# Conformer convolution on one core: six channel tiles convolved by TensorE from shifted copies, and w_mod tiles shared out anew

## The chip, the cores and the metric

The kernel runs on 1 core of one Trainium2 chip. The metric is the device time of that core for one execution, in microseconds (us).

## What is computed

A trunk of two layers over 256 positions and 2048 channels, all in float32. The change lies in layer 0, whose mixer is the conformer module:

```python
def conformer_conv(u, w_pw1, b_pw1, w_dw, b_dw, ln_g, ln_b, w_pw2, b_pw2):
    v = u @ w_pw1 + b_pw1                      # 2048 -> 4096
    a, gt = jnp.split(v, 2, axis=-1)
    v = a * jax.nn.sigmoid(gt)
    v = causal_dwconv(v, w_dw, b_dw)           # 31 taps, each channel by itself
    v = jax.nn.silu(layernorm(v, ln_g, ln_b))  # over the 2048 channels
    return v @ w_pw2 + b_pw2

sc = jax.nn.silu(c)
for i in range(2):
    mod = (sc @ w_mod[i] + b_mod[i])[:, None, :]          # w_mod[i]: 2048 x 12288
    sh1, sc1, g1, sh2, sc2, g2 = jnp.split(mod, 6, axis=-1)
    u = rmsnorm(h, norm_mix_g[i]) * (1 + sc1) + sh1
    h = h + g1 * mix(u)                                   # conformer, then Mamba-2
    u = rmsnorm(h, norm_mlp_g[i]) * (1 + sc2) + sh2
    h = h + g2 * sq_relu_mlp(u, mlp_w1[i], mlp_w2[i])
return rmsnorm(h, final_norm_g)
```

## The kernel before

Activations lie transposed: 128 channels on the partitions, the 256 positions along the row. The 2048 channels are 16 **tiles** of 128, in four groups of four.

**First pointwise product** (`native`, L635). Its 4096 output columns are eight blocks; block b holds the halves a and gate of tiles 2b and 2b + 1. Blocks 0 to 2 run together, blocks 3 to 7 one by one, each in four quarters with a weight of 1 MB (16 products at L649; a float32 product stands as two records in the profile). When a block ends, `glu` (L563) writes its two gated tiles into a ring of 12 padded tiles, `vpad`, in the spare half of the buffers `u`.

**Convolution** (`conv`, L572). The first tile's begins at block 3; from block 4 on, three tiles go into each block. A tile's 31 taps are shared: ScalarE multiplies 24 (L580), four at a time into one wide buffer; VectorE adds the wide buffers (five adds of 128 x 1024, L596), adds seven taps by itself (L599) and folds the four lanes into one (L603, L605). For tiles 14 and 15 TensorE does 13 taps with diagonal weights (L592), ScalarE 12 and VectorE 6. `close` (L608) subtracts the channel mean of tile 0 (made at L614 between the second and the third quarter of block 3; L617), so that later sums stay small, and squares the result.

**Normalisation.** `moments` (L624, L631) sums tiles and squares of a group over the channels, with products of 32 output columns, four of them beside each other; groups 0 to 2 go this way. L730 adds the three groups' rows, L737 the four tiles of the last group; VectorE reads the mean off the bank (L740), and `normed` turns group after group into what the second product reads.

**Second pointwise product** (`outer` and `block`, products at L355). Its weights are split into a high part (ScalarE, L340) and a low part (VectorE, L342).

**w_mod.** The gate and shift vectors are needed step by step, so their matrix (96 MB a layer) is streamed all along in 1 MB **w_mod tiles** of 128 columns, `gemv`. On VectorE a tile is one multiply and sum (L271); on TensorE it is four products of 32 output columns with the conditioning vector as weight (L262), and after four tiles a row copy by ScalarE (L268) and a **turn** of the row into columns (four transposes, L283). `PE_GROUPS` names the groups of tiles that TensorE does, `EARLY` sets the order of the tiles, and `pump(n)` starts n of them: 16 in the 20 quarters of blocks 3 to 7 (`RATE_PW1`), 8 between the products (`BETWEEN`), 16 in the second product (`RATE_PW2`), 8 in the opening of the MLP (`RATE_OPEN`). G1 is the gate behind the conformer, SC2 and SH2 scale and shift ahead of the MLP; each has four groups of four tiles.

**Order of the work.** SyncE (SP) issues all weight loads from one queue in program order (`stream`, L324), each when its buffer is free: `w32` has 3 buffers, `wm` 2, `hid` 4, `acc` 5. On the other engines a scheduler orders by program order and priority: `high_priority(n)` moves an instruction ahead, `issue_after(x)` puts it behind x. PSUM has six banks `mm` and two `ms`.

Of the kernel before, what the change touches and what calls it, by code (L numbers as in the profile page):

```python
# [29 lines left out]
def spread(n, slots):  # L30
# [17 lines left out]
BETWEEN = 8  # L48
# [47 lines left out]
def layout(inp):  # L96
# [5 lines left out]
    head[:HEADS, 1] = a["mb_a_log"].reshape(-1)  # L102
    par = np.concatenate([
# [3 lines left out]
        _cols(a["cf_b_dw"]), _cols(a["cf_ln_g"]), _cols(a["cf_ln_b"]), _cols(a["cf_b_pw2"]),  # L107
# [22 lines left out]
    return {  # L130
        "diag": diag,
# [5 lines left out]
        "pw1": _tiles(pw1), "pw2": _tiles(a["cf_w_pw2"][0]),  # L137
# [23 lines left out]
class Trunk:  # L161
# [368 lines left out]
    def conformer(self):  # L530
# [32 lines left out]
        def glu(ct, bank):  # L563

            with self.tc.high_priority(AHEAD_GLU):
# [3 lines left out]
                nc.vector.scalar_tensor_tensor(out=vpad[ct % 12][:, TAPS - 1:], in0=bank[:, :T],  # L569
                                               scalar=self.col("b_pw1", ct), in1=sg, op0=ALU.add, op1=ALU.mult)  # L570

        def conv(ct):  # L572
# [4 lines left out]

# [9 lines left out]
            if few:  # L587
                i = ct - (NT - DIAG)
                part = (self.bank(self.mm, "mm") if i else self.bank(self.ms, "ms"))[:, :T]
                with self.tc.issue_after(self.pe):  # L590
                    for k in range(PE_TAPS):
                        nc.tensor.matmul(part, lhsT=diag[i][:, k, :], rhs=vp[:, k:k + T], start=k == 0,  # L592
                                         stop=k == PE_TAPS - 1)
# [12 lines left out]
            return y  # L606

        def close(ct, y):  # L608
# [26 lines left out]
        def native(blocks, done, pump=None, hook=None):  # L635
# [67 lines left out]
        native([FIRST], glu, pump=pump, hook=lambda: close(0, y))  # L703
        ct = 1
        for b in range(FIRST + 1, 8):
            for _ in range(3):
                close(ct, conv(ct))
                ct += 1
            if b >= 6:
                moments(b - 6)  # L710
            if b == 7:
                self.rings = ("wm", "hid")
                diag = []
                for i in range(DIAG):
                    diag.append(self.b("hid", [P, PE_TAPS, P]))
                    self.stream(diag[i], a["diag"][i])
# [582 lines left out]
```

## Time and profile before

| | |
|---|---|
| median of 3 runs | 2610.97 us (2608.09 to 2614.57) |
| profiled execution, time | 2609.13 us |
| its span | 2607.2 us, mean granted clock 0.988 |
| TensorE busy (PE) | 2541.3 us, 97% |
| weight loads (PEld) | 2180.5 us, 84% |
| VectorE busy (DVE) | 1945.7 us, 75% |
| ScalarE busy (ACT) | 1363.9 us, 52% |
| moved by DMA | 659.10 MB, mean 253 GB/s |

The profiled execution lies 1.8 us under the median. Times in the rows below are microseconds from the start of the span. PEclk is the share of full speed that TensorE's clock was granted, where 1.00 is 2.4 GHz. SPq is SyncE issuing a DMA. `mm` and `ms` are PSUM banks, `wm` and `hid` buffers of w_mod tiles, `w` a weight, `acc` and `sq` a closed tile and its square. A busy share near 1 of TensorE in a stretch says that it sets the pace there; a bracket at a row's end gives the idle time ahead of it and what ended it.

### The profile page before, as it was taken

What the parts mean: (1) busy time and instruction counts of PE and PEld (TensorE: products, weight loads), DVE (VectorE), ACT (ScalarE), POOL (GpSimd) and SP (SyncE); (2) the same over time, 40 slices, a digit from 0 to 9 for tenths busy, and PEclk for the clock granted to TensorE, in tenths of its full rate; (3) what the DMA queues carried; (4) which work ended last, traced back from release to release, by engine and by line L of the source; (5) the groups of instructions that cost most, each with busy time, mean ns of one, the idle gap of its engine ahead of it and who ended that gap; (6) DMA issues with size and microseconds to landing.
All of it is one profiled execution on the core that took longest, in us unless ns stands there. A gap on an engine that the chain in (4) does not pass through costs nothing.

```text
span 2607.2 us, 36320 instructions
## 1 busy us (share of the span) xinstructions
PE 2541.3 (97%) x14291; PEld 2180.5 (84%) x14291; DVE 1945.7 (75%) x2558; ACT 1363.9 (52%) x2145; POOL 132.5 (5%) x170
## 2 busy tenths in 40 slices
PE   6999999999999999999999999999999999999998
PEld 4877798888888888888888888888998888888886
DVE  6689977677888878887877777888885565565565
ACT  2099754444434434447777666744454344443443
POOL 0000000000000000000000000000000101101000
PEclk8999999999999999999999999999999999999999
DMA  9876797588888888866555455688775555555553
GB/s 406 345 278 252 279 376 285 218 337 320 314 323 328 314 307 334 312 225 220 182 188 184 166 182 182 234 305 317 285 263 189 192 193 190 185 191 194 187 186 144
DMA packets 92878, 659.10 MB, mean 253 GB/s; under 512 B 10497, under 2 KB 10497, under 8 KB 14753
## 3 DMA queue, kind: packets, MB, share of 16 engines
q1 hardware_dynamic: 89138, 644.53, 65.6%
q0 software_dynamic: 3136, 10.59, 1.4%
q8 instruction: 112, 1.84, 0.3%
q10 hardware_dynamic: 432, 1.66, 0.2%
q14 instruction: 60, 0.49, 0.1%
HBM read 654.53 MB, written 2.20 MB: 252 GB/s over the span
## 4 chain that ended last, share of the span: by engine, by line
PE 87%; DVE 6%; DMA 3%; ACT 2%; issue 1%; POOL 0%; ACTq 0%; DVEq 0%; SPq 0%; POOLq 0%
PE mm L355 57%; PE mm L409 8%; PE mm L411 8%; PE mm L410 8%; PE mm L649 3%; ACT taps L580 2%; DMA hid<-wmT 1%; DVE taps L596 1%; DVE wl L342 1%; DVE taps L599 1%; DMA wm<-wmT 1%; DVE hid L271 1%; DVE wm L271 1%; PE ms L262 1%; DMA t<-eac_d 0%
## 5 line engine op out<-in xcount | busy, mean ns | idle before, releaser
L355 PE MATMUL mm<-u,wh 128*128 128x512 f32 (+1 forms) x4544 | 1376.1, 365 | 6.9 <-ACT u L467 3.4
L342 DVE TENSOR_TENSOR wl<-w,wh 128x1024 fp32r<-128x1024 f32 x768 | 940.7, 1228 | 513.5 <-ACT wh L340 510.3
L340 ACT CAST wh<-w 128x1024 fp32r<-128x1024 f32 x768 | 806.8, 1051 | 980.6 <-PE mm L355 602.5
L355 PE MATMUL mm<-u,wl 128*128 128x256 f32 x3840 | 1078.9, 282 | 0.1
L355 PEld LDWEIGHTS mm<-u,wh 128*128 128x128 f32 x4544 | 812.8, 190 | 160.2 <-issue 12.8
L355 PEld LDWEIGHTS mm<-u,wl 128*128 128x128 f32 x3840 | 729.8, 190 | 6.6 <-issue 2.5
L409 PE MATMUL mm<-wh,hid 128*128 128x512 f32 x896 | 350.7, 391 | 0.0
L411 PE MATMUL mm<-wh,hid 128*128 128x512 f32 x896 | 348.8, 389 | 0.0
L410 PE MATMUL mm<-wl,hid 128*128 128x512 f32 x896 | 348.7, 389 | 0.0
L271 DVE SCALAR_TENSOR_TENSOR wm<-wm,scb 128x2048 f32<-128x2048 f32 x128 | 292.3, 2283 | 8.2 <-DMA wm<-wmT 8.2
L649 PE MATMUL mm<-u,w 128*128 128x256 f32 x1024 | 232.3, 388 | 26.7 <-ACT u L560 25.1
L649 PEld LDWEIGHTS mm<-u,w 128*128 128x128 f32 x1024 | 197.6, 195 | 64.9 <-ACT u L560 26.6
L409 PEld LDWEIGHTS mm<-wh,hid 128*128 128x128 f32 x896 | 168.2, 188 | 35.7 <-issue 1.0
L410 PEld LDWEIGHTS mm<-wl,hid 128*128 128x128 f32 x896 | 168.2, 188 | 35.4 <-issue 0.7
L411 PEld LDWEIGHTS mm<-wh,hid 128*128 128x128 f32 x896 | 168.2, 188 | 35.2
L355 PE MATMUL mm<-hid,wh 128*128 128x512 f32 (+1 forms) x576 | 182.5, 373 | 2.4 <-DVE acc L837 2.4
L580 ACT ACTIVATE taps<-u,par 128x256 f32<-128x256 f32 x360 | 148.2, 500 | 3.6 <-DVE taps L596 2.2
L355 PE MATMUL mm<-hid,wl 128*128 128x256 f32 x512 | 143.8, 281 | 0.0
L355 PEld LDWEIGHTS mm<-hid,wh 128*128 128x128 f32 x576 | 104.1, 188 | 23.1 <-DVE acc L837 2.7
L299 POOL TENSOR_TENSOR mod<-mod,par 128x4 f32<-128x4 f32 x46 | 39.8, 864 | 1319.3 <-DVE wm L271 885.1
L355 PEld LDWEIGHTS mm<-hid,wl 128*128 128x128 f32 x512 | 96.9, 189 | 0.4 <-issue 0.2
L596 DVE TENSOR_TENSOR taps<-taps,taps 128x1024 f32<-128x1024 f32 x74 | 90.1, 1218 | 8.7 <-ACT taps L580 7.8
(241 smaller groups left out, 1562.9 us busy)
## 6 DMA issues: line engine op xcount, KB each, us to landing
w<-w SPq DMA_DIRECT2D x256, 1024.0 KB, 4.9
wm<-wmT SPq DMA_DIRECT2D x140, 1024.0 KB, 7.0
w<-win SPq DMA_DIRECT2D x80, 1024.0 KB, 4.9
hid<-wmT SPq DMA_DIRECT2D x52, 1024.0 KB, 10.6
w<-pw SPq DMA_DIRECT2D x48, 1024.0 KB, 5.3
w<-wout SPq DMA_DIRECT2D x32, 1024.0 KB, 6.9
acc<-ac_d POOLq DMA_DIRECT2D x16, 512.0 KB, 7.7
h<-xT SPq DMA_DIRECT2D x4, 512.0 KB, 6.2
```

The costliest lines, as they stand in the source:

```text
L262: self.pe = nc.tensor.matmul(self.row_sums[32 * t:32 * t + 32, :], lhsT=self.scol[:, kt:kt + 1].broadcast_to([P, 32]), rhs=w[:, t * 512:(t ...
L271: self.sum = nc.vector.scalar_tensor_tensor(out=w, in0=w, scalar=1.0, in1=self.scb, op0=ALU.mult, op1=ALU.mult, accum_out=m[:, i:i + 1]).ins
L299: nc.gpsimd.tensor_tensor(out=m, in0=m, in1=b, op=ALU.add)
L340: nc.scalar.copy(out=wh, in_=w[:, s, :])
L342: nc.vector.tensor_tensor(out=wl, in0=w[:, s, :], in1=wh.bitcast(F32), op=ALU.subtract)
L355: self.pe = self.nc.tensor.matmul(out, lhsT=lhsT, rhs=rhs, skip_group_check=True, **kw).ins
L409: mm(banks[q], lhsT=hi, rhs=wh[:, k, :], start=g == 0 and t == 0, stop=False)
L410: mm(banks[q], lhsT=hi, rhs=wl[:, k, :], start=False, stop=False)
L411: mm(banks[q], lhsT=lo, rhs=wh[:, k, :], start=False, stop=g == 3 and t == 3)
L580: st["tap"] = nc.scalar.activation(out=p4[:, q, :], in_=vp[:, k + q:k + q + T], func=AF.Identity, scale=self.col("w_dw", ct * TAPS + k + q ...
L596: nc.vector.tensor_add(wide, wide, products(four("wl"), k))
L649: self.pe = nc.tensor.matmul(o, lhsT=w[:, t, j * P:(j + 1) * P], rhs=u[g][:, t, :], start=g == 0 and t == 0 and j < 2, stop=g == 3 and t == 3,
```

## The change

1. **Six tiles are convolved by TensorE, all 31 taps** (`TE_ROWS`: tiles 3, 4, 5, 13, 14, 15; a *convolved tile*). `shift` copies the padded tile four times by DMA, each 8 positions on: 128 rows of 263 values become 32 partitions with four channels each (*copies*: 512 pieces of 1,052 bytes a tile). `weigh` loads the tile's weights (0.5 MB). `convolve` makes 32 products: a product takes 32 channels, a quarter of the output partitions, and four taps, which are 8 apart. The last tap, the 32nd, is zero, so padded tiles are one column longer. `close` takes the result from PSUM and adds the bias in the same instruction. The channels of these six tiles come out permuted; the parameters and the rows of pw2 are permuted to match.
2. **Weights and copies have one buffer each** (`quad` on `acc`, `copies` on `xpad`) for tiles 3, 4, 5, 13 and 14; tile 15 has its own. They are asked for at quarter 2 of blocks 3, 4 and 5 and quarter 3 of block 7; the convolution stands in quarter 3, ahead of its products. Half of the copies of tiles 14 and 15 is issued from ScalarE's queue.
3. **The other ten tiles** have 28 taps on ScalarE (six adds) and three on VectorE.
4. **The end of the conformer is written out:** FILL (three w_mod tiles), convolution 14, moments of group 2, sums of tiles 12 and 13, convolution 15, the row of sums, sums of 14 and 15, mean.
5. **w_mod:** only SH2's tiles are TensorE's now, G1's are VectorE's; `EARLY` brings SH2's first eight tiles forward, and three tiles are started in FILL, five in BETWEEN.

```diff
-BETWEEN = 8
+FILL, BETWEEN = 3, 5
-ACT_TAPS = 24
-DIAG, PE_TAPS, FEW_TAPS = 2, 13, 12
-EARLY = [(0, s, g) for s, g in ((G1, 0), (G1, 1), (G1, 2), (SC2, 0), (G1, 3), (SH2, 0), (SC2, 1), (SH2, 1), (SC2, 2),
-                               (SH2, 2), (SC2, 3), (SH2, 3))]
-PE_GROUPS = {(0, G1, g) for g in range(4)} | {(0, SH2, g) for g in range(4)}
+ACT_TAPS = 28
+TE_ROWS = (3, 4, 5, 13, 14, 15)
+LONG = T + 7
+EARLY = [(0, s, g) for s, g in ((G1, 0), (G1, 1), (G1, 2), (SC2, 0), (SH2, 0), (SH2, 1), (G1, 3), (SC2, 1), (SH2, 2),
+                               (SC2, 2), (SH2, 3), (SC2, 3))]
+PE_GROUPS = {(0, SH2, g) for g in range(4)}
...
+    taps = np.zeros((32, D), f)
+    taps[:TAPS] = a["cf_w_dw"][0].reshape(TAPS, D)
+    quad = np.zeros((len(TE_ROWS), 4, 32, 8, 4, 32), f)
+    for i, ct in enumerate(TE_ROWS):
+        w = taps[:, ct * P:(ct + 1) * P].reshape(4, 8, 32, 4)
+        for p in range(32):
+            quad[i, :, p, :, :, p] = w[:, :, p, :]
...
-        W = T + TAPS - 1
+        W = T + TAPS
...
+            nc.gpsimd.memset(v[:, W - 1:], 0.0)
...
+        quad = self.b("acc", [P, 8, P], bufs=5)
+        copies = self.xpad[:, :4 * LONG].rearrange("p (c t) -> p c t", c=4)
...
+        def weigh(ct, w):
+            self.stream(w, a["quad"][TE_ROWS.index(ct)])
+        def shift(ct, r):
+            for i in range(4):
+                dst, src = r[32 * i:32 * i + 32], vpad[ct % 12][:, 8 * i:8 * i + LONG]
+                if ct >= NT - 2 and i % 2:
+                    with self.tc.high_priority(AHEAD_CHAIN):
+                        nc.scalar.dma_start(out=dst, in_=src)
+                else:
+                    self.stream(dst, src)
+        def convolve(ct, w, r):
+            o = parts[ct] = self.bank(self.mm, "mm")[:, :T]
+            with self.tc.issue_after(self.pe):
+                for k in range(8):
+                    for c in range(4):
+                        self.pe = nc.tensor.matmul(o[32 * c:32 * c + 32, :], lhsT=w[:, k, 32 * c:32 * c + 32],
+                                                   rhs=r[:, c, k:k + T], start=k == 0, stop=k == 7,
+                                                   skip_group_check=True).ins
...
+            if ct in parts:
+                self.sub = nc.vector.scalar_tensor_tensor(out=d, in0=parts[ct], scalar=self.col("b_dw", ct),
+                                                          in1=st["m0"], op0=ALU.add, op1=ALU.subtract).ins
...
+                    if row and g == (3 if row == 13 else 2):
+                        weigh(row, quad)
+                        shift(row, copies)
                     load(0, g)
                     self.pump(pump(g))
+                    if row and g == 3:
+                        convolve(row, quad, copies)
+                        if row == 13:
+                            weigh(14, quad)
                     products(0, g, 0, 4)
...
+        native([FIRST], glu, pump=pump, hook=lambda: close(0, y), row=3)
+        for b, rows in ((4, (1, 2, 3)), (5, (4, 6, 7)), (6, (5, 8, 9)), (7, (10, 11, 12))):
+            for ct in rows:
+                close(ct, None if ct in parts else conv(ct))
             if b >= 6:
                 moments(b - 6)
...
+            native([b], glu, pump=pump, row={4: 4, 5: 5, 7: 13}.get(b))
+        there = [self.load_w(a["pw2"][0, 0])]
+        self.side = self.ms, "ms"
+        with self.tc.issue_after(self.pe):
+            self.pump(FILL)
...
+        shift(14, copies)
+        quad15 = self.wp.tile([P, 8, P], F32, tag="wh", name=self.nm("taps"), bufs=3)
+        weigh(15, quad15)
+        copies15 = self.b("hid", [P, 4, LONG])
+        shift(15, copies15)
+        there.append(self.load_w(a["pw2"][1, 0]))
+        close(13, None)
+        convolve(14, quad, copies)
         moments(2)
...
+        with self.tc.issue_after(self.pe):
+            direct(12, first=True)
+            direct(13)
+        convolve(15, quad15, copies15)
+        close(14, None)
+        close(15, None)
...
+            direct(14)
+            direct(15)
```

How instructions stand on three engines shows what the text of the diff does not. On VectorE at the start of the convolution, where tile 0 is summed (`taps_595` and `taps_609` are tile 0's wide buffer, `taps_746` and `taps_790` tile 1's), the order was:

```order
L596 TENSOR_TENSOR taps_595<-taps_595,taps_618 128x1024
L596 TENSOR_TENSOR taps_595<-taps_595,taps_624 128x1024
L599 SCALAR_TENSOR_TENSOR taps_595<-u_161,par,taps_595 128x256 x7
L596 TENSOR_TENSOR taps_746<-taps_746,taps_751 128x1024
L603 TENSOR_TENSOR taps_595<-taps_595 128x512
L596 TENSOR_TENSOR taps_746<-taps_746,taps_757 128x1024
L605 TENSOR_TENSOR taps_595<-taps_595 128x256
L596 TENSOR_TENSOR taps_746<-taps_746,taps_763 128x1024
L596 TENSOR_TENSOR taps_746<-taps_746,taps_769 128x1024
L617 TENSOR_TENSOR acc_177<-taps_595,ssum_687 128x256
```

There, seven taps follow the last add of tile 0. The same place on VectorE is now, with `wm_677` a w_mod tile:

```order
L604 TENSOR_TENSOR taps_609<-taps_609,taps_632 128x1024
L282 SCALAR_TENSOR_TENSOR wm_677,mod_679<-wm_677,scb 128x2048
L604 TENSOR_TENSOR taps_609<-taps_609,taps_638 128x1024
L604 TENSOR_TENSOR taps_609<-taps_609,taps_644 128x1024
L607 SCALAR_TENSOR_TENSOR taps_609<-u_162,par,taps_609 128x256 x3
L604 TENSOR_TENSOR taps_790<-taps_790,taps_795 128x1024
L609 TENSOR_TENSOR taps_609<-taps_609 128x512
L604 TENSOR_TENSOR taps_790<-taps_790,taps_801 128x1024
L611 TENSOR_TENSOR taps_609<-taps_609 128x256
L604 TENSOR_TENSOR taps_790<-taps_790,taps_807 128x1024
L651 TENSOR_TENSOR acc_190<-taps_609,ssum_699 128x256
```

The seven single taps of tile 0 have become three, the adds one more, and a w_mod tile of 128 x 2048 stands between them, ahead of the two folds (L609, L611) that end tile 0's sum.

On TensorE in the tail, the rows from the last moments' tiles to the second product were (`hid_1643` and `hid_1645` are diagonal weights, `t_268` the row of sums):

```order
L631 MATMUL ms_1379<-sq_1539,ones 32x256
L631 MATMUL ms_1379<-sq_1586,ones 32x256
L592 MATMUL ms_1806<-u_161,hid_1643 128x256 x13
L592 MATMUL mm_1851<-u_162,hid_1645 128x256 x13
L730 MATMUL mm_1894<-t_268_1849,bT_116 128x512
L737 MATMUL mm_1894<-acc_180,ones 128x256
L737 MATMUL mm_1894<-lo_1633,ones 128x256
L737 MATMUL mm_1894<-acc_180,ones 128x256
L737 MATMUL mm_1894<-nrm_1804,ones 128x256
L737 MATMUL mm_1894<-acc_180,ones 128x256
L737 MATMUL mm_1894<-lo_1847,ones 128x256
```

Both convolutions stood together there, ahead of all sums. TensorE's rows are now, from the last quarter of block 7 on (`acc_194` is `quad`, `xpad` its copies; the first L634 is tile 13, then 14, then 15):

```order
L634 MATMUL mm_1684<-xpad,acc_194 32x256 x32
L683 MATMUL mm_1605<-u_165,w_239_1676 128x256 x8
L683 MATMUL mm_1606<-u_165,w_239_1676 128x256 x8
L273 MATMUL ms_1745<-hid_1742,scol 32x512 x4
L273 MATMUL ms_1745<-hid_1750,scol 32x512 x4
L273 MATMUL ms_1745<-wm_1756,scol 32x512 x4
L634 MATMUL mm_1780<-xpad,acc_194 32x256 x32
L665 MATMUL ms_1351<-acc_192,ones 32x256 x4
```

Three w_mod tiles (L273) stand ahead of convolution 14 where the moments stood. Behind four more rows of moments TensorE goes on with the first sums of the last group:

```order
L773 MATMUL mm_1823<-acc_193,ones 128x256
L773 MATMUL mm_1823<-lo_1595,ones 128x256
L773 MATMUL mm_1823<-acc_193,ones 128x256
L773 MATMUL mm_1823<-nrm_1778,ones 128x256
L634 MATMUL mm_1828<-hid_1770,taps_1768 32x256 x32
L784 MATMUL mm_1823<-t_255_1821,bT_117 128x512
L773 MATMUL mm_1823<-acc_193,ones 128x256
L773 MATMUL mm_1823<-lo_1862,ones 128x256
```

The sums of tiles 12 and 13 now stand ahead of convolution 15, the row of sums and those of tiles 14 and 15 behind it.

On SyncE's queue, from the last quarter of block 7 on, the loads were:

```order
L326 DMA w_251_1719<-pw 128x2048
L326 DMA wm_1721<-wmT 128x2048
L326 DMA w_275_1896<-pw 128x2048
L326 DMA w_276_1898<-pw 128x2048
L326 DMA w_277_1900<-pw 128x2048
L326 DMA hid_1941<-wmT 128x2048
L326 DMA wm_1949<-wmT 128x2048
```

They are weights and w_mod tiles alone. SyncE's loads are now:

```order
L337 DMA acc_194<-quad 128x1024
L337 DMA xpad<-u_162 32x4x263 x4
L337 DMA w_239_1676<-pw 128x2048
L337 DMA wm_1678<-wmT 128x2048
L337 DMA acc_194<-quad 128x1024
L337 DMA w_244_1740<-pw 128x2048
L337 DMA hid_1742<-wmT 128x2048
L337 DMA hid_1750<-wmT 128x2048
L337 DMA wm_1756<-wmT 128x2048
L337 DMA xpad<-u_162 32x4x263 x2
L337 DMA taps_1768<-quad 128x1024
L337 DMA hid_1770<-u_163 32x4x263 x2
L337 DMA w_252_1775<-pw 128x2048
```

Where three pw2 weights and the w_mod tiles stood, the weights of tile 14 (the second `acc_194`) stand ahead of a pw2 weight, three w_mod tiles and half of tile 14's copies (the second `xpad`).

## Rows read from the trace of the kernel before

**Rows 1.** Busy time by stretch: us, busy of each engine, PEclk, DMA share, GB/s.
```profile
131.00:293.00 162.00, 160.34 (x814) 127.74 (x812) 153.40 (x234) 154.84 (x385) 8.03 (x9) 1.00 0.67 257
293.00:320.00 27.00, 22.25 (x128) 14.66 (x120) 23.34 (x41) 17.89 (x40) 0.00 (x0) 1.00 0.80 316
320.00:425.00 105.00, 104.99 (x858) 95.28 (x858) 75.35 (x97) 52.62 (x80) 7.83 (x10) 1.00 0.91 360
```

**Rows 2.** Timeline of TensorE, the tail: start, us, line, [idle before <-releaser].
```profile
292.23 0.64 PE L631 MATMUL ms<-acc,ones 128*32 128x256 f32 x8
292.69 0.61 PE L631 MATMUL ms<-sq,ones 128*32 128x256 f32 x8
293.23 5.88 PE L592 MATMUL ms<-u,hid 128*128 128x256 f32 x26
...
310.02 0.70 PE L737 MATMUL mm<-acc,ones 128*128 128x256 f32 x2 [1.84 <-DVE acc L617]
...
317.89 1.06 PE L262 MATMUL ms<-wm,scol 128*32 128x512 f32 x8 [2.30 <-DMA wm<-wmT]
...
320.01 0.39 PE L355 MATMUL mm<-u,wh 128*128 128x256 f32 x1 [0.62 <-DVE u L465]
```

**Rows 3.** Timeline of VectorE, the tail.
```profile
309.54 0.42 DVE L617 TENSOR_TENSOR acc<-taps,ssum 128x256 f32<-128x256 f32 x1
...
311.20 0.42 DVE L740 TENSOR_SCALAR a<-mm 128x256 f32<-128x256 f32 x1
```

**Rows 4.** Timeline of TensorE, blocks 3 to 7.
```profile
135.90 7.14 PE L649 MATMUL mm<-u,w 128*128 128x256 f32 x32 [1.66 <-DMA w<-pw]
142.97 1.06 PE L262 MATMUL mm<-wm,scol 128*32 128x512 f32 x8
143.97 7.17 PE L649 MATMUL mm<-u,w 128*128 128x256 f32 x32
...
191.81 0.66 PE L283 MATMUL mm<-ident,t 128*128 128x128 f32 x4
```

**Rows 5.** Groups by line, 318 to 425 us: weight loads of w_mod (busy, mean ns).
```profile
L262 PEld LDWEIGHTS ms<-hid,scol 128*32 128x32 f32 x48 | 0.9, 106 | 0.8
```

**Rows 6.** Timeline of VectorE, tile 0.
```profile
141.56 1.23 DVE L596 TENSOR_TENSOR taps<-taps,taps 128x1024 f32<-128x1024 f32 x1 [0.37 <-ACT taps L580]
...
144.42 2.86 DVE L599 SCALAR_TENSOR_TENSOR taps<-u,par,taps 128x256 f32<-128x256 f32 x7
...
150.07 0.42 DVE L605 TENSOR_TENSOR taps<-taps 128x256 f32<-128x256 f32 x1
```

**Rows 7.** Groups by line of VectorE, 131 to 320 us.
```profile
L596 DVE TENSOR_TENSOR taps<-taps,taps 128x1024 f32<-128x1024 f32 x74 | 90.1, 1218 | 8.7 <-ACT taps L580 7.8
L599 DVE SCALAR_TENSOR_TENSOR taps<-u,par,taps 128x256 f32<-128x256 f32 x110 | 45.1, 477 | 0.4
...
L271 DVE SCALAR_TENSOR_TENSOR hid<-hid,scb 128x2048 f32<-128x2048 f32 x2 | 4.6, 2281 | 0.0
```

**Rows 8.** Groups by line of ScalarE, 131 to 320 us.
```profile
L580 ACT ACTIVATE taps<-u,par 128x256 f32<-128x256 f32 x360 | 148.2, 500 | 3.6 <-DVE taps L596 2.2 <-DVE u L569 1.5
```

**Rows 9.** The page's DMA queues, and one issue in SyncE's timeline.
```profile
q1 hardware_dynamic: 89138, 644.53, 65.6%
q0 software_dynamic: 3136, 10.59, 1.4%
...
313.08 0.33 SPq L326 DMA_DIRECT2D wm<-wmT  x1
```

**Rows 10.** TensorE by slices; six slices from 430 to 436, first and last.
```profile
316.00:318.00 2.00, 0.11 (x4) 1.00 1.00 406
...
430.00:431.00 1.00, 0.39 (x2) 0.50 0.44 90
...
435.00:436.00 1.00, 1.00 (x7) 0.50 0.99 418
```

**Rows 11.** w_mod's products alone (L262) in the second product.
```profile
320.00:425.00 105.00, 10.64 (x80) 1.56 (x80) 1.00 0.91 360
```

More of the change, by code (lines that the diff above doesn't have):

```diff
@@ L102, in layout @@
     head[:HEADS, 1] = a["mb_a_log"].reshape(-1)
+    order = np.arange(D).reshape(NT, P)
+    for ct in TE_ROWS:
+        order[ct] = order[ct].reshape(32, 4).T.reshape(-1)
+    order = order.reshape(-1)
     par = np.concatenate([
@@ L106, in layout @@
         a["cf_w_dw"][0].reshape(TAPS, NT, P).transpose(2, 1, 0).reshape(P, -1),
-        _cols(a["cf_b_dw"]), _cols(a["cf_ln_g"]), _cols(a["cf_ln_b"]), _cols(a["cf_b_pw2"]),
+        *(_cols(np.asarray(a[n]).reshape(-1)[order]) for n in ("cf_b_dw", "cf_ln_g", "cf_ln_b")), _cols(a["cf_b_pw2"]),
         a["mb_conv_w"][0].reshape(4, 48, P).transpose(2, 1, 0).reshape(P, -1),
@@ L136, in layout @@
         "wmT": wmt,
-        "pw1": _tiles(pw1), "pw2": _tiles(a["cf_w_pw2"][0]),
+        "pw1": _tiles(pw1), "pw2": _tiles(a["cf_w_pw2"][0][order]),
         "wdt": np.ascontiguousarray(wdt.reshape(NT, P, P).transpose(1, 0, 2)),
@@ L586, in conv @@
             four = lambda tag: self.wp.tile([P, 4, T], F32, tag=tag, name=self.nm("taps"), bufs=3)
[L587 to L593, printed above, removed]
             wide = products(four("wh"), k0)
@@ L633, in moments, with native @@
                                          skip_group_check=True)
-        def native(blocks, done, pump=None, hook=None):
+        def native(blocks, done, pump=None, hook=None, row=None):
             banks = [[self.bank(self.mm, "mm") for _ in range(2)] for _ in blocks]
@@ L710, in conformer @@
                 moments(b - 6)
[L711 to L716, printed above, removed]
-            native([b], glu, pump=pump)
+            native([b], glu, pump=pump, row={4: 4, 5: 5, 7: 13}.get(b))
[3 more added lines that the diff above has]
+            self.pump(FILL)
@@ L718, in conformer @@
         with self.tc.issue_after(st["gate"]):
             nc.scalar.activation(out=self.t("rcol", [P, 2])[:, :1], in_=self.eps, func=AF.Sqrt)
-        moments(2)
-        while ct < NT:
-            close(ct, conv(ct))
-            ct += 1
-            if ct == NT - 1:
-                rows = self.t("t2", [P, 2 * T], bufs=3)
-                nc.scalar.copy(out=rows, in_=st["sums"])
+        shift(14, copies)
+        quad15 = self.wp.tile([P, 8, P], F32, tag="wh", name=self.nm("taps"), bufs=3)
@@ new lines, in conformer, with direct @@
+        weigh(15, quad15)
[4 more added lines that the diff above has]
+        convolve(14, quad, copies)
+        moments(2)
+        rows = self.t("t2", [P, 2 * T], bufs=3)
+        nc.scalar.copy(out=rows, in_=st["sums"])
+        ps = self.bank(self.mm, "mm")
+        def direct(i, first=False):
+            for e in range(2):
+                self.pe = nc.tensor.matmul(ps[:, e * T:(e + 1) * T], lhsT=self.ones, rhs=st["sq"][i][e],
+                                           start=first and e == 0, stop=i == NT - 1, skip_group_check=True).ins
@@ L727, in conformer @@
+        with self.tc.issue_after(self.pe):
[4 more added lines that the diff above has]
+        close(15, None)
         tap, d15 = st["tap"], self.sub
-        ps = self.bank(self.mm, "mm")
         with self.tc.issue_after(self.pe):
-            nc.tensor.matmul(ps, lhsT=self.sel, rhs=rows, start=True, stop=False, skip_group_check=True)
-        there = [self.load_w(a["pw2"][b, 0]) for b in range(3)]
+            nc.tensor.matmul(ps, lhsT=self.sel, rhs=rows, start=False, stop=False, skip_group_check=True)
@@ L734, in conformer @@
         with self.tc.high_priority(AHEAD_CHAIN):
-            for i in range(12, NT):
-                for e in range(2):
-                    self.pe = nc.tensor.matmul(ps[:, e * T:(e + 1) * T], lhsT=self.ones, rhs=st["sq"][i][e], start=False,
-                                               stop=i == NT - 1, skip_group_check=True).ins
+            direct(14)
+            direct(15)
             mean, var, msq = (self.t("a", [P, T], bufs=3) for _ in range(3))
@@ L773, in conformer @@
             half = self.split_half(there[0], 0, tap, d15)
-        self.side = self.ms, "ms"
         with self.tc.issue_after(self.pe):
             self.pump(BETWEEN)
+        there.append(self.load_w(a["pw2"][2, 0]))
         self.rings = ("wm", "hid", "hid")
@@ L987, in mamba @@
         self.time_steps(u)
-        self.xpad = [self.one.tile([P, 3 + T], F32, tag=f"xpad{i}", name=f"xpad{i}") for i in range(5)]
+        self.xpad = [self.xpad[:, i * (3 + T):(i + 1) * (3 + T)] for i in range(5)]
         for v in self.xpad:
```

26 lines of the change are left out of this document (8 added, 18 removed).

## The prediction

> **What bounds the kernel now.** I read the busy time by stretch first: it says which engine sets the pace in each stage. From 131 to 293 us, the first pointwise product with its gate and the convolution, TensorE is busy 160 of 162 us while VectorE and ScalarE are busy 153 and 155 [rows 1]: three engines run level. From 320 to 425 us, the second pointwise product, TensorE alone is full and VectorE has 30 us to spare [rows 1]. Between them lies the **tail**, which this change is about, so I read TensorE's timeline there: its last block of products ends at 292.23, then it convolves 13 taps of tiles 14 and 15 (from 293.23), waits 1.84 us for VectorE's last tile, starts the last sums at 310.02, and goes over to the second product at 320.01 [rows 2]. VectorE's timeline shows why: it closes tile 15 at 309.54 and takes the mean at 311.20 [rows 3]. So ahead of the tail the price of an edit is its time on TensorE; in the tail it is what the last two tiles wait for; after 320 it is TensorE again.
>
> My zero, Z, is the end of block 7 on TensorE, 292.23 before. The mean was taken at Z + 19.0, the second product ran at Z + 27.8.
>
> **Blocks 3 to 7 (136 to 292 us).** TensorE loses the twelve w_mod tiles of G1's groups 0 to 2, 1.00 us each from the start of one to the products behind it [rows 4], 12.0 us; and three turns of a row into columns, 0.5 each (the one at 191.81 and its like) [rows 4], 1.5 us. It gains four convolved tiles (3, 4, 5, 13). No row has this convolution, but the moments have its shape: products of 32 output columns over 256 positions, four side by side. Their first eight records start at 292.23, the next eight at 292.69 [rows 2]: 0.46 us for four products. A tile has 32 products, eight such rounds, 3.7 us; four tiles 14.8. Upper bound, if the four did not run side by side: 64 records at 0.22 (32 records in 7.1 us) [rows 4], 14 us a tile. I take 3.7, the nearest row; w_mod tiles, with four different weights, run side by side too. Net **+1.3 us**.
>
> A rule speaks against it. In the moments' rows sixteen records with sixteen weight loads of about 0.11 us [rows 5] pass in 0.92 us, so the loads hide. The Trainium skill ("TensorE: Matmul & The Clock Gate", Part 3 on packing small matmuls) says that a weight load overlaps running products only when its row group differs, and products placed side by side by output columns share theirs. By it the loads would add up, as in the third rival below; no run here has these very weights.
>
> A new wait comes with it. TensorE makes the mean of tile 0 after the second quarter of block 3, and all its work queues behind. Before, tile 0 was summed at 150.5 [rows 6], and TensorE, held 1.00 by a w_mod tile, asked at 151. Now it asks at 135.90 + 2 x 7.04 = 150.0 [rows 4]. VectorE has six adds and three taps now instead of five and seven, but a w_mod tile stands between adds 4 and 5 (order of VectorE). Add 4 ends at 142.8 [rows 6]; w_mod tile 2.3 [rows 7] to 145.1; two adds to 147.4; three taps at 0.41 [rows 7] to 148.6; and the four instructions that then end the sum took 147.2 to 150.5 before [rows 6], so 151.9 now. ScalarE's four extra taps, 0.41 each [rows 8], are done by then. TensorE stands **+2.0 us**; bounds 0, if the w_mod data let the adds go first on time, and 3.
>
> VectorE and ScalarE are relieved: ten tiles instead of fourteen and two part ones. Adds and taps of VectorE: 10 x (6 x 1.22 + 3 x 0.41) = 85 us against 135 [rows 7], plus twelve w_mod tiles, 27. ScalarE: 280 taps, 115 us against 148 [rows 8]. None of it shortens the path: TensorE's 156 us cover both, and VectorE's added w_mod tiles with them. Copies and weights of tiles 3, 4, 5 and 13, 1 MB a tile, are asked for a quarter block or more ahead with the DMA engines at 0.67 [rows 1]: nothing. So Z moves by +3.3.
>
> **The tail.** SP's queue sets it. The weights of tile 14 reuse tile 13's buffer, so SP waits for convolution 13, which ends one quarter block, 7.0 us, before Z. Behind it stand a pw2 tile, three w_mod tiles (FILL) and half of tile 14's copies. One megabyte alone, issued at 313.08, was of use to TensorE at 317.89, 4.8 us [rows 2, 9]; each further one adds 2.5 us at 418 GB/s [rows 10]. With 4.7 MB the third w_mod tile is there at Z - 6.7 + 2.3 + 11.3 = Z + 6.9. Meanwhile ScalarE's queue sends its half of the copies through the same engines. A copied tile is 512 pieces of 1,052 bytes. Lower bound by bytes: q1's mean packet is 7,231 bytes and 307 ns (65.6% of 16 engines' span, by its 89,138 packets), so 45 ns. Upper bound: q0's mean packet, 3,377 bytes, 186 ns [rows 9]. The line through the two gives 113 ns, which I take: 512 x 113 / 16 engines = 3.6 us a tile, 1.8 a queue. ScalarE's halves put the third w_mod tile off to some Z + 9, and tile 14's last copies follow 1.8 later: Z + 10.8. TensorE's order is FILL, convolution 14, moments, sums of 12 and 13, convolution 15, the rest: until Z + 10.8 it has only FILL's 3 us to do.
>
> From there: convolution 14 3.7, moments 0.9, sums of 12 and 13 1.8 (eight records at 0.22), to Z + 17.2; tile 15's weights and copies, 4 us behind tile 14's, are there; convolution 15 3.7; the row of sums and the sums of 14 and 15, 2.6, with closing and squaring 15 alongside. Mean at **Z + 23.4 against Z + 19.0: +4.4**. With pieces at 45 ns it is +2.3, at 186 ns +9.5; if TensorE never waited, its own work is 15.7 and the term -3.3. From the mean to the second product 8.8 us stay.
>
> **The second product.** Ten w_mod tiles stood in TensorE's way there, 80 records [rows 11]; the new order leaves five (one of BETWEEN, four of SH2's third group): **-5.0**. Three turns before, three now. VectorE gets four more tiles, 9 us, where it has 30 free [rows 1]; the last stands just ahead of the last evacuation and could cost up to 1 us. In the MLP's opening the same eight tiles change places: 0, bounds -0.5 and 2. Zeroing one more column per padded tile fills idle GpSimd time: 0.
>
> **Sum:** 1.3 + 2.0 + 4.4 - 5.0 = +2.7 on the profiled execution, 2609.13 to 2611.8. The median of the three runs, 2610.97, lies 1.8 above it: 2613.7. A measurement of this kernel can tell about 0.3%, 7.8 us, from no change: this is no change.
>
> **Rivals.**
> *TensorE's clock falls in the tail.* From Z to Z + 10.8 it would have 3 us of work. Before, after short products with waits between them from 425 on, its granted clock was 0.50, the 1.2 GHz level, in the six slices from 430 to 436 [rows 10], with 5.3 us of work in them: 2.6 us lost. Against it: with 0.11 us of work in 316 to 318 the clock stayed at 1.00, 2.4 GHz [rows 10]. If it falls: 2613.7 + 2.6 = 2616.3.
> *TensorE hardly waits.* Pieces are cheap, ScalarE's queue brings tile 14 early, tile 0 is summed in time: 1.3 + 0 - 3.3 - 5.0 = -7.0, 2604.0. For it: VectorE, which held the tail before [rows 3], is free there.
> *Loads don't hide.* 64 loads of 0.11 in the open beside each tile's products: 7 us a tile, 42 for six: 2656. The rows speak against it. That is the time which the rule on packing would give.
> *Small pieces are dear (slower).* At 186 ns tile 14's copies land near Z + 16 and the mean is at Z + 28.5: 2618.8. That is the point from which it is slower by over 0.3%; at q1's 307 ns it would be some 2625. For it: no transfer here has pieces of this size; against: in these rows fewer bytes always took less.
> *It doesn't do what it says:* VectorE still ends last, its new w_mod tiles held up by late data; the mean stays near Z + 19, 2609.
>
> **How the numbers follow.** Forecast 0.36, clock 0.16, TensorE hardly waits 0.32 (half of it beyond 7.8 us, as I may have its waits and bounds too high together), dear pieces 0.10, loads 0.02, VectorE last 0.04. Faster by over 0.3%: 0.16; slower: 0.10 + 0.02 = 0.12; the same: 0.72. The range takes in the clock, both bounds of the pieces and most of the second rival, down to 3 to 4 us below its 2604: 2600 to 2619.
>
> **What would show it.** On TensorE: 64 records of a convolved tile in 3.7 us; 2 us idle ahead of the mean of tile 0, ended by VectorE; block 7 ending near 295.5; then short waits ended by w_mod transfers and one ahead of convolution 14 ended by a copy; the mean near 319; five w_mod tiles in the second product instead of ten. Wrong would be a convolved tile far from 3.7 us, waits of the tail ended by VectorE, or a second product in which TensorE waits for VectorE.

## The result and the profile after

The changed kernel took **2612.82 us** (median of 22 runs, 2609.81 to 2616.17), the kernel before 2608.91 us (22 runs): ratio 1.0014, 95% interval 1.0008 to 1.0021, some 3.9 us slower. That is the forecast sign and size (+2.7, 2613.7 us, no change to speak of), inside the range, though not by the forecast's terms alone. The profiled executions lie further apart, 2615.12 and 2609.13 us, with spans of 2613.3 and 2607.2, so the stages below sum to +6.1.

TensorE's timeline after (columns as in [rows 2]) shows block 3 and the tail:

```profile
135.38 14.05 PE L683 MATMUL mm<-u,w 128*128 128x256 f32 x64 [1.49 <-DMA w<-pw]
151.69 0.92 PE L644 MATMUL ms<-taps,ones 128*128 128x256 f32 x2 [2.26 <-DVE taps L611]
152.41 8.58 PE L683 MATMUL mm<-u,w 128*128 128x256 f32 x32
160.91 3.67 PE L634 MATMUL mm<-xpad,acc 128*32 128x256 f32 x64
...
288.82 7.17 PE L683 MATMUL mm<-u,w 128*128 128x256 f32 x32
297.58 1.06 PE L273 MATMUL ms<-hid,scol 128*32 128x512 f32 x8 [1.59 <-DMA hid<-wmT]
300.07 1.06 PE L273 MATMUL ms<-hid,scol 128*32 128x512 f32 x8 [1.43 <-DMA hid<-wmT]
305.34 1.93 PE L273 MATMUL ms<-wm,scol 128*32 128x512 f32 x8 [4.20 <-DMA wm<-wmT]
309.62 5.04 PE L634 MATMUL mm<-xpad,acc 128*32 128x256 f32 x64 [2.35 <-DMA xpad<-u]
314.47 0.62 PE L665 MATMUL ms<-acc,ones 128*32 128x256 f32 x8
...
317.38 3.67 PE L634 MATMUL mm<-hid,taps 128*32 128x256 f32 x64
...
330.54 0.80 PE L366 MATMUL mm<-u,wh 128*128 128x256 f32 x2 [1.84 <-ACT u L475]
```

Z, the end of block 7, is 295.96. A convolved tile takes 3.6 us (160.91 to 164.52). The wait for tile 0's mean is there, 2.26 us, ended by VectorE; but the quarter behind it takes 8.58 us instead of 7.1. In the tail each w_mod product waits for its transfer, and what follows the longest of these waits runs slower: 1.93 us where a w_mod tile had taken 1.06, 5.04 where a convolved tile had taken 3.67. The stretches say why (columns as in [rows 1], the engines in the order TensorE, weight loads, VectorE, ScalarE, GpSimd):

```profile
149.40:152.40 3.00, 0.74 (x3) 0.60 (x3) 3.00 (x5) 2.66 (x7) 0.00 (x0) 0.94 1.04 431
152.40:161.00 8.60, 8.60 (x37) 7.04 (x39) 7.16 (x11) 8.35 (x22) 0.00 (x0) 0.82 1.00 415
161.00:164.60 3.60, 3.60 (x65) 1.94 (x65) 3.05 (x4) 3.60 (x11) 0.00 (x0) 1.00 0.80 294
305.30:307.30 2.00, 1.93 (x8) 0.20 (x8) 0.00 (x0) 0.00 (x0) 0.00 (x0) 0.50 0.44 56
309.60:314.50 4.90, 4.88 (x68) 2.81 (x72) 0.00 (x0) 0.00 (x0) 0.10 (x1) 0.71 1.04 287
330.50:336.00 5.50, 4.07 (x16) 3.56 (x16) 5.50 (x9) 4.78 (x9) 0.00 (x0) 0.50 1.03 426
```

The clock was granted at a mean of 0.82 behind the wait for the mean, at 0.50, the 1.2 GHz level, and a mean of 0.71 in the tail, and again at 0.50 at the start of the second product: three times, each behind a wait or idle stretch of TensorE. And this is what the tail waited for, the chain of waits (start, us, what):

```profile
292.39 2.21 DVE wm L282 x2
...
295.85 0.49 DVE u L585
...
296.36 10.26 DMA xpad<-u
...
306.64 2.74 DMA xpad<-u
...
309.62 5.04 PE mm L634 x62
314.66 0.86 PE ms L665 x16
...
323.87 0.44 DVE a L791
```

The chain comes from VectorE: behind a w_mod tile and the closing of tile 13 it writes the gate of tile 14 (L585) only at 295.85, and no copy of tile 14 can be issued before that. From 296.36 a copy is then under way for 10.26 us and after it another for 2.74. SyncE's waits from 255 to 312 us (us in total, times, longest) name the link between the two copies, and its timeline shows both in one row:

```profile
SPq L337 <- DVE u L585: 13.7, 2, 12.4
...
SPq L337 <- DMA xpad<-u: 9.6, 1, 9.6
SPq L337 <- PE mm L634: 8.1, 1, 8.1
```

```profile
296.36 10.83 SPq L337 DMA_DIRECT2D xpad<-u  x2
```

SyncE stood 9.6 us between its two copies of tile 14 until a copy of ScalarE's had landed. The program gives its DMAs eight completion counters over and over, and this copy's counter had last gone to that one, so it must wait for it though the two write different rows. The DMA engines were full for most of that time and ran nearly empty only at its end, as their share in the stretches shows (the last column but one):

```profile
296.00:302.00 6.00, 2.13 (x16) 0.31 (x16) 0.81 (x2) 3.00 (x4) 0.00 (x0) 1.00 1.03 381
302.00:306.00 4.00, 0.66 (x4) 0.20 (x8) 0.00 (x0) 0.00 (x0) 0.00 (x0) 0.53 1.01 194
306.00:308.00 2.00, 1.27 (x8) 0.00 (x0) 0.00 (x0) 0.00 (x0) 0.00 (x0) 0.50 0.22 46
```

The DMA view from 296 to 312 us gives packets, MB and share of each queue, and KB and us to landing of each transfer; q10 is ScalarE's:

```profile
q10 hardware_dynamic: 576, 0.54, 20.7%
...
xpad<-u SPq DMA_DIRECT2D x2, 131.5 KB, 6.7
xpad<-u ACTq DMA_DIRECT2D x2, 131.5 KB, 10.3
```

ScalarE's 576 packets took 20.7% of 16 engines' 16 us, 92 ns each. Only 512 of them are pieces (512 x 1,052 bytes are all of the 0.54 MB), so a piece cost between 92 and 104 ns and pieces were not dear; yet ScalarE's copies took 10.3 us to land, beside the w_mod tiles ahead of them.

| stage | before | after | gained or lost |
|---|---|---|---|
| start of block 3 to Z | 156.3 | 160.6 | +4.3 |
| Z to mean | 19.0 | 27.9 | +8.9 |
| mean to the second product's steady run | 8.8 | 8.9 | 0 |
| second product | 105.3 | 102.5 | -2.8 |
| to the MLP's second product | 107.6 | 102.2 | -5.4 |
| rest, and what lies ahead of block 3 | | | +1.1 |

The last row says nothing: behind the MLP's opening the traces of these kernels lie up to 8 us apart.

### The profile page after: what moved, and what is told of

The parts are those of the page before. It is cut to its first block, busy times and chain, and to the rows that moved or that the text cites. A ratio compares the mean times of both kernels' runs of the same rounds, so it can differ in the third digit from the quotient of the medians.

```text
span 2613.3 us, 36583 instructions
## 1 busy us (share of the span) xinstructions
PE 2539.6 (97%) x14479; PEld 2180.9 (83%) x14479; DVE 1930.8 (74%) x2478; ACT 1328.9 (51%) x2061; POOL 127.8 (5%) x182
## 4 chain that ended last, share of the span: by engine, by line
PE 85%; DVE 6%; ACT 4%; DMA 4%; issue 1%; POOL 0%; ACTq 0%; DVEq 0%; SPq 0%
PE mm L366 56%; PE mm L420 8%; PE mm L422 8%; PE mm L421 8%; ACT taps L595 3%; PE mm L683 2%; DMA hid<-wmT 1%; DVE taps L604 1%; DVE hid L282 1%; DVE wl L353 1%; DVE wm L282 1%; DMA wm<-wmT 1%; DMA t<-eac_d 1%; DMA xpad<-u 0%; PE ms L1263 0%
## 5 line engine op out<-in xcount | busy, mean ns | idle before, releaser
L282 DVE SCALAR_TENSOR_TENSOR wm<-wm,scb 128x2048 f32<-128x2048 f32 x134 | 306.0, 2284 | 8.9 <-DMA wm<-wmT 8.6
L595 ACT ACTIVATE taps<-u,par 128x256 f32<-128x256 f32 x280 | 114.7, 500 | 7.1 <-DVE u L585 7.1
L282 DVE SCALAR_TENSOR_TENSOR hid<-hid,scb 128x2048 f32<-128x2048 f32 x42 | 95.7, 2285 | 25.8 <-DMA hid<-wmT 25.7
```

The costliest lines, as they stand in the source:

```text
L282: self.sum = nc.vector.scalar_tensor_tensor(out=w, in0=w, scalar=1.0, in1=self.scb, op0=ALU.mult, op1=ALU.mult, accum_out=m[:, i:i + 1]).ins
L595: st["tap"] = nc.scalar.activation(out=p4[:, q, :], in_=vp[:, k + q:k + q + T], func=AF.Identity, scale=self.col("w_dw", ct * TAPS + k + q ...
```

## The experiments

Each was timed beside the kernel before; differences are between medians, in us, against the changed kernel's 2612.82 unless said otherwise. The kernel before had medians from 2608.91 to 2610.27 in these groups of runs, so a difference can be off by up to 1.4 us; the ratios to the kernel before are free of that (the changed kernel's is 1.0014, 1.0008 to 1.0021).

**The wait at the mean.** The mean is asked for one quarter later.

```diff
-                    if hook and g == 2:
+                    if hook and g == 3:
```


> Edit: the changed kernel, with the mean of tile 0 asked for ahead of the fourth quarter of block 3 instead of the third, 7 us later. Theory (the wait for tile 0's sum costs its 2.26 us and, behind it, a fallen TensorE clock that makes the next quarter 8.58 instead of 7.1 us): no wait at the mean, no slow quarter, block 7 ends some 3.7 us earlier after its start, and the time falls by 3 to 4 us against the changed kernel. Rival (the wait is cover for something else, a transfer or the convolution of tile 3 that would be late next): the wait moves to the convolution of tile 3 and the time stays within 1 us.

2608.94 us, **-3.9** (ratio to before 1.0000, 0.9991 to 1.0009). No wait, no slow quarter. The wait cost its 2.26 us and, by the clock, 1.5 more.

Is the w_mod tile between VectorE's adds the cause? Here the mean stays, and the tile goes.

```diff
-RATE_PW1 = spread(16, 20)
+RATE_PW1 = [0, 0] + spread(16, 18)
```


> Edit: the changed kernel, with the first w_mod tiles of blocks 3 to 7 started later (none in block 3's first three quarters; still 16 in all), so that none stands between VectorE's adds of tile 0. The mean stays ahead of the third quarter. Theory (that one w_mod tile of 2.3 us makes TensorE wait 2.26 us for tile 0's sum, and the wait lowers its clock): the wait falls under 0.5 us, the next quarter takes 7.1 us again, and the time falls by 3 to 4 us against the changed kernel, as in e1_mean_later. Rival (the sum of tile 0 is late for ScalarE's products, not for the w_mod tile): the wait stays at 2 us and the time within 1 us.

2610.80 us, **-2.0** (ratio to before 0.9999, 0.9990 to 1.0008, not told apart from e1_mean_later). TensorE's timeline shows the cause confirmed and new waits further on:

```profile
149.47 0.59 PE L644 MATMUL ms<-taps,ones 128*128 128x256 f32 x2
149.90 7.07 PE L683 MATMUL mm<-u,w 128*128 128x256 f32 x32
...
282.71 3.67 PE L634 MATMUL mm<-xpad,acc 128*32 128x256 f32 x64 [1.42 <-DMA xpad<-u]
...
306.87 6.46 PE L634 MATMUL mm<-xpad,acc 128*32 128x256 f32 x64 [2.69 <-DMA xpad<-u]
```

The mean is asked for at 149.47 without a wait, and the quarter takes 7.07; but tile 13's convolution now waits 1.42 us for its copies, and convolution 14, at the fallen clock, takes 6.46. Whether that costs time against the later mean, the medians do not tell.

**Two queues for the copies, or one.** All copies from SyncE:

```diff
-                if ct >= NT - 2 and i % 2:
+                if False:
```


> Edit: the changed kernel, with all copies of tiles 14 and 15 issued from SyncE's queue, none from ScalarE's. Theory (ScalarE's small pieces take turns with the large packets of the w_mod tiles, land after 10 us, and SyncE's third copy waits 9.6 us for one of them): copies land about 3 us behind the third w_mod tile, convolution 14 starts 3 to 4 us earlier than at Z + 13.7, and the time falls by 2 to 4 us. Rival (pieces of 1,052 bytes are dear by themselves on whichever queue): convolution 14 starts at Z + 13 to 15 and the time stays within 1.5 us. Second rival (SyncE's queue becomes late for tile 15 and the weights behind it): convolution 15 waits for its copies, and the time rises by 2 us or more.

2611.55 us, **-1.3** (ratio to before 1.0010, 1.0002 to 1.0019), not told apart from the changed kernel. Convolution 14 starts at Z + 11.5 instead of 13.7, part of the way that the theory gives it, and the mean comes 2.4 us earlier behind Z; the second product, 1.9 us longer in this trace, gives most of it back. The time settles nothing. The Trainium skill ("DMA: Bandwidth & Descriptors", Issuing engines are not separate DMA queues) says that a second issuing engine saves issue time only; these runs agree, as two queues were not faster than one, and the trace adds that the second can cost the counter's wait.

**FILL ahead of tile 14's weights**, so that SyncE need not wait for convolution 13 before it:

```diff
                     if row and g == 3:
                         convolve(row, quad, copies)
-                        if row == 13:
-                            weigh(14, quad)
...
             self.pump(FILL)
+        weigh(14, quad)
```


> Edit: the changed kernel, with the request for tile 14's weights moved behind the pw2 weight and the three w_mod tiles of FILL on SyncE's queue; nothing else moves. Theory (the wait for convolution 13's end, some 8 us on SyncE's queue, is what puts FILL's transfers into the tail): FILL's products run without a wait, convolution 14 starts near Z + 7 instead of Z + 13.7, the mean comes near Z + 20, and the time falls by 6 to 8 us. Rival (the DMA engines are full at 0.97 of the tail, so whatever comes first delays the rest): the second product starts where it did, within 2 us, held by the w_mod tiles between, and the time falls by less than 2 us.

2607.96 us, **-4.9** (ratio to before 0.9993, 0.9985 to 1.0002), less than the 6 to 8 expected. FILL's waits are gone but for one of 1.13 us; convolution 14 starts at Z + 8.9, later than I had it, behind 4.82 us for its copies. The edit did a second thing: the counters fall otherwise, and SyncE issues its two copies of tile 14 one right behind the other (its row, and TensorE's):

```profile
297.52 1.20 SPq L337 DMA_DIRECT2D xpad<-u  x2
```

```profile
305.48 5.43 PE L634 MATMUL mm<-xpad,acc 128*32 128x256 f32 x64 [4.82 <-DMA xpad<-u]
```

So the 4.9 hold FILL's place and the counter's wait together; how they share it was not tried.

**Both**, the later mean and FILL first:

> Edit: the edits of e1_mean_later and e3_fill_first together, on the changed kernel. Theory (the two losses lie at different places, block 3 and the tail, and add up: 3.9 and 4.9 us): the time is 8 to 9 us under the changed kernel, near 2604. Rival (what ends earlier in block 3 is given back in the tail, where transfers decide): no better than e3_fill_first alone, 2608.

2598.11 us, **-14.7** (ratio to before 0.9954, 0.9940 to 0.9968): 5.9 more than the two by themselves (5.3 if each is taken against the kernel before in its own runs, little more than the noise of four medians). The traces bear it out: from Z to the mean it is 27.9 us in the changed kernel, 28.2 with the later mean alone, 23.5 with FILL first alone, 16.4 with both. TensorE's tail:

```profile
292.39 1.92 PE L273 MATMUL ms<-hid,scol 128*32 128x512 f32 x16
294.13 1.04 PE L273 MATMUL ms<-wm,scol 128*32 128x512 f32 x8
295.96 3.67 PE L634 MATMUL mm<-xpad,acc 128*32 128x256 f32 x64 [0.80 <-DMA xpad<-u]
...
302.35 3.67 PE L634 MATMUL mm<-hid,taps 128*32 128x256 f32 x64
```

No FILL product waits, convolution 14 starts at Z + 3.5 and takes 3.67 us. Where do the 5.9 come from? With the later mean alone, SyncE's waits from 255 to 312 us are:

```profile
SPq L337 <- PE mm L634: 14.9, 1, 14.9
...
SPq L337 <- DVE u L585: 5.6, 1, 5.6
```

The wait for tile 13's gate (L585) has fallen from 12.4 us to 5.6, but SyncE then stands 14.9 for convolution 13 (L634), ahead of tile 14's weights. With FILL first alone it is the other way round, 3.2 for convolution 13 and up to 13.0 for the gate:

```profile
SPq L337 <- DVE u L585: 20.5, 2, 13.0
```

Each edit removes or shortens one of two waits on the queue, and the other stays. The next run has FILL first, and rids the mean of its wait as e9_no_early_tile does, with the mean in its old place:

> Edit: the edits of e9_no_early_tile and e3_fill_first together, on the changed kernel. It asks why e5_mean_and_fill won 5.9 us more than its two edits by themselves. Theory (moving the mean also brought the gate of tile 13 forward on ScalarE and VectorE by some 7 us, and with it tile 13's copies, behind which all transfers of the tail stand on SyncE's queue; without the mean's wait but with the late gate the transfers still run into the tail): the gate of tile 13 is still waited for some 13 us on SyncE's queue, convolution 14 starts at Z + 7 to 10, not Z + 3.5, and the time is 2604 to 2608. Rival (the wait at the mean and the clock behind it are all that counts): convolution 14 starts near Z + 3.5 and the time is 2598 to 2600.

2607.75 us, **-5.1** (ratio to before 0.9992, 0.9983 to 1.0001): the time is as expected, and convolution 14 starts at Z + 11.1, later still than the 7 to 10 expected. SyncE's waits in e12_tile_and_fill, then in e5_mean_and_fill:

```profile
SPq L337 <- DVE u L585: 24.7, 2, 16.4
```

```profile
SPq L337 <- DVE u L585: 10.1, 2, 5.8
```

SyncE waits 16.4 us for the gate of tile 13 (VectorE, L585) before it can issue that tile's copies, and every transfer of the tail stands behind them; with the later mean it waits 5.8. VectorE's timelines show this gate and, in the second row, that of tile 14:

```profile
277.44 0.48 DVE L585 SCALAR_TENSOR_TENSOR u<-mm,par,a 128x256 f32<-128x256 f32 x1 [0.20 <-ACT a L583]
...
296.35 0.48 DVE L585 SCALAR_TENSOR_TENSOR u<-mm,par,a 128x256 f32<-128x256 f32 x1 [0.85 <-ACT a L583]
```

```profile
266.49 0.48 DVE L585 SCALAR_TENSOR_TENSOR u<-mm,par,a 128x256 f32<-128x256 f32 x1 [1.42 <-ACT a L583]
...
289.55 0.48 DVE L585 SCALAR_TENSOR_TENSOR u<-mm,par,a 128x256 f32<-128x256 f32 x1 [3.64 <-ACT a L583]
```

Tile 13's gate came 17 us ahead of Z in the one, 26 ahead in the other. Tile 14's came 1.9 us behind Z in the one and 2.9 ahead in the other: convolution 14 starts 7.6 us earlier behind Z, and 4.8 of them are this gate, the rest faster transfers. In all five runs with the later mean tile 13's gate lies between 265 and 268 us, in all others with six convolved tiles and the new sharing between 276 and 279. So moving the mean also set VectorE's and ScalarE's work in another order, and the lost wait alone does not make the two worth more together. That the order does is read from these traces; e12_tile_and_fill also moves w_mod tiles, and which of the reordered instructions counts was not tried.

**Further on this line.** All copies on SyncE as well:

> Edit: the edits of e1_mean_later, e3_fill_first and e2_one_queue together, on the changed kernel. Theory (with the w_mod tiles out of the way, what convolution 14 still waits for is that ScalarE's copies of tile 15 share the DMA engines with tile 14's, and that SyncE's third copy waits for one of ScalarE's; in one queue tile 14's 512 pieces go first, some 3 us at about 95 ns a piece): convolution 14 starts near Z + 6 instead of Z + 8.9, and the time is 2 to 3 us under that of e5_mean_and_fill, near 2601.5. Rival (SyncE needs 0.6 us for each copy, so that one queue is as late as two): within 1 us of e5_mean_and_fill.

2600.05 us (2596.59 to 2603.98), not told apart from e5_mean_and_fill, where 2 to 3 less were expected; convolution 14 starts at Z + 3.5 in both. Four w_mod tiles in FILL:

```diff
-FILL, BETWEEN = 3, 5
+FILL, BETWEEN = 4, 4
```


> Edit: the kernel of e5_mean_and_fill, with four w_mod tiles in FILL and four between mean and second product instead of three and five. Theory (the fourth tile's transfer fits into block 7, where the DMA engines are at 0.55 of the last 6 us, and its product into the 0.8 us wait ahead of convolution 14; behind the mean one w_mod transfer less is waited for): 0 to 2 us under e5_mean_and_fill. Rival (its transfer lies ahead of tile 14's weights and copies and puts them off by 2.5 us): 1 to 3 us above e5_mean_and_fill.

2599.01 us (ratio to before 0.9957, 0.9945 to 0.9970): no gain either. Five convolved tiles:

```diff
-TE_ROWS = (3, 4, 5, 13, 14, 15)
+TE_ROWS = (3, 4, 13, 14, 15)
...
-            native([b], glu, pump=pump, row={4: 4, 5: 5, 7: 13}.get(b))
+            native([b], glu, pump=pump, row={4: 4, 7: 13}.get(b))
```


> Edit: the kernel of e5_mean_and_fill, with five tiles convolved by TensorE instead of six (tile 5 goes back to ScalarE and VectorE). Theory (TensorE sets the pace of blocks 3 to 7 and a convolved tile costs it 3.6 us; ScalarE with 124 of 156 us and VectorE with 138 have room for one more tile of 11.5 and 8.6): 3 to 4 us under e5_mean_and_fill. Rival (ScalarE is full in block 6, and the gate of tile 13 comes late again, with its copies and the transfers behind them): 2 us or more above e5_mean_and_fill.

**2592.35 us**, 5.8 under e5_mean_and_fill, where 3 to 4 were expected, and 0.9926 (0.9912 to 0.9939) of the kernel before: it beats both. Blocks 3 to 7, in the stretches of the two (e5_mean_and_fill first):

```profile
135.80:292.40 156.60, 156.56 (x933) 130.11 (x933) 138.00 (x165) 124.29 (x311) 6.76 (x9) 1.00 0.82 292
```

```profile
137.10:289.60 152.50, 152.46 (x866) 128.25 (x866) 144.72 (x176) 135.43 (x338) 5.76 (x9) 1.00 0.79 293
```

TensorE is full in both; the tile taken off it shortens them by 4.1 us, and VectorE and ScalarE have the room. The rest of the 5.8 was not traced.

**The sharing of w_mod.** The old order at the end of `EARLY`:

```diff
-                               (SC2, 2), (SH2, 3), (SC2, 3))]
+                               (SC2, 2), (SC2, 3), (SH2, 3))]
```


> Edit: the changed kernel, with the last two groups of w_mod in the old order (SC2's third group ahead of SH2's). Theory (the opening of the MLP won 4 to 5 us because a w_mod product of SH2 now stands in TensorE's wait for the first normalised tile, costs nothing there and lets the clock rise 3 us sooner, and VectorE's four tiles no longer delay the normalised tiles): with the old order the wait ahead of the first product of the MLP is back at 1.4 us and more, and the time rises by 3 to 5 us. Rival (the gain is from elsewhere, from evacuations that end earlier): the time stays within 1 us.

2617.10 us, **+4.3**. In TensorE's waits from 438 to 546 us the opening's are back:

```profile
PE mm L366 <- ACT u L478: 2.4, 2, 1.3
...
PE mm L366 <- DVE u L479: 0.6, 2, 0.4
```

One of ScalarE's two, 1.31 us, stands ahead of the first product; the other, 1.09, which I had not named, at 505.48, right behind the turn of SH2's last row at 503.79. After the change neither is there. The opening takes 106.9 us in this trace and 102.2 after the change, so the order is worth 4.8 of the 5.4 in the table; in the other traces it takes 102 to 104 with the new order and 107.6 or more with the old.

The sharing alone, in the kernel before, with the new `EARLY`:

```diff
-PE_GROUPS = {(0, G1, g) for g in range(4)} | {(0, SH2, g) for g in range(4)}
+PE_GROUPS = {(0, SH2, g) for g in range(4)}
```


> Edit: the kernel before, with the new order and sharing of w_mod tiles alone (G1 on VectorE; SH2 brought forward). Theory (the sharing pays only because the convolution frees VectorE and ScalarE): VectorE, busy 153 of 162 us in blocks 3 to 7, gets 27 us more and sets the pace there; blocks 3 to 7 and the tail become some 15 us longer though TensorE is relieved of 13.5, the second product and the opening of the MLP win 3 and 5: 5 to 10 us slower than the kernel before. Rival (VectorE's tiles find room beside the tail's w_mod tiles that are gone from TensorE): within 2 us of the kernel before or faster.

2624.22 us, 14.7 over the kernel before (2609.50 in the same runs), more than I gave it: TensorE waits 24 us for VectorE's closed tiles (11.5 ahead of the moments, 12.8 ahead of the last sums).

The convolution alone, the changed kernel with the old `EARLY`:

```diff
-PE_GROUPS = {(0, SH2, g) for g in range(4)}
+PE_GROUPS = {(0, G1, g) for g in range(4)} | {(0, SH2, g) for g in range(4)}
```


> Edit: the changed kernel, with the old order and sharing of w_mod tiles (G1 on TensorE). Theory (the convolution alone gives TensorE 14.4 us in blocks 3 to 7 that are not taken off elsewhere, and a longer tail; the order in the opening of the MLP is the old one): blocks 3 to 7 take 171 us instead of 160.6, the second product and the opening lose 3 and 5 us: 15 to 20 us slower than the changed kernel. Rival (the blocks had slack in their transfers that hides it): under 5 us slower than the changed kernel.

2632.39 us, 19.6 over the changed kernel; blocks 3 to 7 take 171.0 us instead of 160.6. So either half alone loses, 14.7 and 22.9 against the kernel before, and together they lose 3.9: each frees the engine that the other fills.

## Why the prediction was right, step by step

- **Convolved tile, 3.7 us:** 3.6. The rival "loads don't hide" fell: 64 loads at a mean of 109 ns would be 7.0 us in a row and passed within these 3.6. By the Trainium skill's rule on packing ("TensorE: Matmul & The Clock Gate", Part 3) loads of one row group don't overlap running products; the trace shows otherwise for products beside each other by output columns (TensorE is busy 3.60 of 3.60 us from 161.00 to 164.60), and the measurement decides.
- **Wait at the mean, +2.0:** 2.26, and by the w_mod tile, as said. The term missed the clock behind it, 1.5. From the start of block 3 to Z it is 4.3 longer, forecast 3.3.
- **Tail, +4.4:** mis-sized, +8.9. The third w_mod tile was used at Z + 9.4, forecast Z + 9, and a piece cost 92 to 104 ns, taken 113. What failed is "tile 14's last copies follow 1.8 later": the third of them, SyncE's second, waited for a counter that ScalarE's copy held, and convolution 14 started at Z + 13.7 instead of 10.8. In e2_one_queue, without that wait, it starts at Z + 11.5. Most of the rest is the clock on convolution 14, 1.4; the 0.9 on the w_mod tile cost nothing, as TensorE still waited 2.35 us for copies behind it. The forecast also took tile 14's gate to come in time, without a row for it: VectorE wrote it 0.1 us ahead of Z, against 2.9 ahead in e5_mean_and_fill, and what that cost here was not tried. The upper bound at 186 ns, +9.5, was not counted as the forecast was: it has all 6.0 us of ScalarE's two halves ahead of the third w_mod tile, the forecast 2.1 of 3.6; counted alike, I estimate some +7.
- **Clock rival, 2.6 us:** its mechanism came true at three places, not one; in the tail products ran 2.3 us longer, and 1.4 of them counted.
- **Second product, -5.0:** -2.8. Five w_mod tiles fewer, as counted; but the products up to 336 us ran at the low clock, which I estimate at 1.6 (half of the 3.3 us from 332.7 on). The other 0.6 was not traced.
- **MLP's opening, 0, bounds -0.5 and 2:** -5.4, the step that was wrong. I counted that the same eight tiles change places and not what they stand beside: a w_mod product now fills TensorE's wait for the first normalised tile, and the turn of SH2's last row no longer stands late with a wait of 1.09 us behind it (e4_open_swap, +4.3).

So the convolved tile, the wait at the mean and the count of w_mod tiles were right by their mechanism, and the total was right by luck: a gain that was missed, 5.4, paid for a tail that was mis-sized, 4.5.

## What to carry to other kernels

A queue that issues in program order makes each wait the wait of all behind it: ask for what needs nothing ahead of what must wait, and count small copies on a second queue by when they can be issued and land beside large transfers, not by their bytes. Price a wait of TensorE with the slow products behind it. Two edits that move work between the same engines are to be tried together and apart: here each of the change's halves lost, and two small repairs won some 5 us more together than their sum, since each removed one of two waits on the same queue.

## What the runs showed of the hardware

TensorE's granted clock fell to 0.50 behind the tail's wait of 4.20 us and at the start of the second product, and after the wait of 2.26 at the mean the next 8.6 us had a mean of 0.82. Copies of 131.5 KB in pieces of 1,052 bytes landed after 10.3 us beside w_mod tiles; in e5_mean_and_fill, where the engines' share was 0.55 from 286 to 292.5 us, ScalarE's two of tile 14, issued from 290.06 on, landed after 4.0 us, in this row of its DMA view:

```profile
xpad<-u ACTq DMA_DIRECT2D x2, 131.5 KB, 4.0
```
